# A hybrid decoder block: TensorE takes its instructions in the written order, and four places are rearranged for it

## The chip, the core and the metric

One core of a Trainium2 chip runs the whole block as one program. The metric is the device time of an execution in microseconds (us), lower is better. The kernel before was run three times. One more execution was profiled; its trace gives every instruction of every engine. The engines are TensorE (PE, matrix products), VectorE (DVE), ScalarE (ACT), GpSimd (POOL) and SyncE (SP), which here only issues DMAs.

## The reference

512 tokens of width 2048 get 16 meta tokens ahead of them (528 in all). The block is:

```python
u = rmsnorm(h, norm_g)
q, k, v, g_att, z_ssm, xbc, dt, m_att, m_ssm = split(u @ w_in)
oa = rmsnorm(diff_attention(q, k, v, lam), subln_g) * silu(g_att)   # 8 heads, two softmax maps, a = p0 - lam * p1
y_att = oa @ w_br_attn
xs, bm, cm = split(silu(causal_conv4(xbc) + conv_b))
ys = ssd_chunked(xs, softplus(dt + dt_bias), -exp(a_log), bm, cm)   # 4 groups of 8 heads, chunks of 128 tokens
yg = rmsnorm_per_group((ys + xs * d_skip) * silu(z_ssm))
y_ssm = yg @ w_br_ssm
merged = sigmoid(m_att) * y_att + sigmoid(m_ssm) * y_ssm
out = rmsnorm((h + merged @ w_out)[16:], final_g)
```

All of it is float32.

## The kernel before, in words

**The dense products.** Every weight matrix is cut into jobs of 256 output columns. `plan` (L60-87) writes their order: keys and values of the first head, two merge gates and `dt`; then per head a `kv` and a `qg` job; gates `ma` 2 and on; the conv inputs `bc` and `xs`; per SSD group two `z` jobs and two to six gates, the last of them `ms` 7; then eight jobs each of `ya` (attention branch), `ys` (SSD branch) and `out`. Each float32 operand is split in a high and a low part (`wh` by ACT at L173, `wl` by DVE at L174, for the weights; `xsplit`, L438 and L439, for the activations), and a product is three matmuls. Most jobs go through `strassen` (L216-322): seven products P1 to P7 of half-sized blocks in place of eight, two units each, 12 matmuls of 256 or 264 columns a unit (L310). The sums of weight blocks are made at L184 and L187 on DVE, and the results are put together by "posts" at L187. Jobs of form F go through `plain` (L324-361, matmuls at L354). The activation operands have names, B11, B12, B21, B22 and the sums T1 to T4, and `TOK` says which product reads which; they lie in slots of two pools (eight slots `x`, six slots `y`). Weights come in by DMA, five buffers deep (`pump`, L157-167).

**What sets the order.** `dense` (L400) takes a job's units: sums two units ahead, splits (`prep`) so that up to three prepared units wait, and then the matmuls (`run_unit`, L384). Behind each unit `run_posts` runs what `later` has put off by so many units, and `run_side` (L197) takes one step of each of up to three side tasks, which are generators; in the heads a new one may start every 3 units, in the SSD stage every 10. A head's side tasks are queued 6 units behind its `qg` job. `before={j: f}` runs f ahead of the sums of unit j.

**Side tasks.** Per head: `qk_parts` (L684-695) makes the split queries and keys `qs`, `ks`, `kl` in four steps; `attn_rows` (L698-772) makes scores for four blocks of 128 rows (matmuls L719 with 128 rows of contraction and L722 with 64, written as all L719 of a step, then all L722), softmax (L726 to L756), transposes (L762, L764), and values (L770, L771); `attn_out` (L774-800) normalizes (`og`, L792) and transposes (L796). Between the conv stage and the first `z` job, after a `flush`, stands the SSD set-up (L897-961): it loads `dt` (L913), transposes it (L922, L924), computes softplus and decays in a chain on DVE and ACT (L925-946), sums them along the chunk by matmul (L948, L949), and transposes the sums (L958). Per SSD group, `ssd_group` (L984-1119) runs four chunks with matmuls from L1026 to L1108 (L1067 the state, L1086 the output, L1095 ACT, L1101 and L1108 the norm) and operations on POOL (L178, L190) between them.

**Between the stages.** The last gate job, `ms` 7, splits the attention operands (`att_quarter`, L1123) ahead of its units 8 to 11. While `ya` runs, `ssm_operands` (L1194) makes the seven operands of `ys` from `yq`; T2 and T3 are subtracted on POOL (`psub`, L181), the others on DVE (`vsub`, L184). During the last `ys` job `out_operand` (L1225) starts the operands of `out` from `mq`. `final` (L1301-1330) takes the squares' sums of the finished rows by matmul (L1307), the norm (L1309 POOL), spreads it (L1313) and scales (L1319 DVE). At the start `token_scale` (L510-547) takes the same steps for the input norm, in two halves; the second half's matmul L527 is written behind the first dense unit.

**Who orders the engines.** The kernel is built with a planner that orders each engine's instructions by its own estimate of their times:

```python
with tile.TileContext(nc, schedule_with_timeline_sim=True) as tc:
    block_kernel(tc, t_in, out)
```

An engine then runs its list in the planner's order, and waits for semaphores where another engine's result is needed. An instruction written later can so stand earlier on its engine.

## Time and profile before

| What | Value |
|---|---|
| three runs | 1816.68, 1818.43, 1822.35 us; median 1818.43 |
| profiled execution | 1816.67 us, of which the span of the trace 1815.0 us |
| mean granted clock of TensorE in the span | 0.973 of full speed |
| instructions | PE 13547, DVE 3004, ACT 1961, POOL 241 |
| busy | PE 1707.7 us, DVE 1565.0, ACT 969.2, POOL 262.1 |
| moved by DMA | 244.10 MB |

The span runs from the first to the last instruction that the trace has; all times in it count from its start. Busy time is the time in which an engine executed something other than waiting, branching or issuing a DMA. PEclk is the clock granted to TensorE as a share of full speed: 1.00 is 2.4 GHz, 0.50 is 1.2 GHz. Stages by time, roughly: start to 140 us, heads 140 to 600, gates and conv 600 to 846, SSD with its `z` jobs and gates 846 to 1350, `ya` 1350 to 1450, `ys` 1450 to 1612, `out` to the end.

### The profile page before, as it was taken

What the parts mean: (1) busy time and instruction counts of PE and PEld (TensorE: products, weight loads), DVE (VectorE), ACT (ScalarE), POOL (GpSimd) and SP (SyncE); (2) the same over time, 40 slices, a digit from 0 to 9 for tenths busy, and PEclk for the clock granted to TensorE, in tenths of its full rate; (3) what the DMA queues carried; (4) which work ended last, traced back from release to release, by engine and by line L of the source; (5) the groups of instructions that cost most, each with busy time, mean ns of one, the idle gap of its engine ahead of it and who ended that gap; (6) DMA issues with size and microseconds to landing.
All of it is one profiled execution on the core that took longest, in us unless ns stands there. A gap on an engine that the chain in (4) does not pass through costs nothing.

```text
span 1815.0 us, 35924 instructions
## 1 busy us (share of the span) xinstructions
PE 1707.7 (94%) x13547; PEld 1639.2 (90%) x13547; DVE 1565.0 (86%) x3004; ACT 969.2 (53%) x1961; POOL 262.1 (14%) x241
## 2 busy tenths in 40 slices
PE   5999999999999799999998999999998999989995
PEld 4999988988989799999997889989998999989995
DVE  6898878887888699999988888988978499999996
ACT  6555545554565355555576665555553254455553
POOL 0000000000000000000013431121302012235443
PEclk9999989998999899999999999999999999999998
DMA  7332212221223134333556555455466545433433
GB/s 298 134 113 82 88 64 88 70 89 65 88 76 106 66 129 129 129 118 129 154 172 177 172 156 171 158 169 167 127 231 228 186 144 171 153 114 106 139 117 105
DMA packets 136765, 244.10 MB, mean 134 GB/s; under 512 B 15088, under 2 KB 78768, under 8 KB 136080
## 3 DMA queue, kind: packets, MB, share of 16 engines
q1 hardware_dynamic: 136592, 241.81, 40.9%
q8 instruction: 107, 1.75, 0.4%
q14 instruction: 66, 0.54, 0.1%
HBM read 207.88 MB, written 33.88 MB: 133 GB/s over the span
## 4 chain that ended last, share of the span: by engine, by line
PE 68%; DVE 18%; DMA 5%; issue 4%; ACT 4%; POOL 1%; SPq 0%; DVEq 0%; ACTq 0%; POOLq 0%
PE d_ps L310 53%; PE d_ps L354 6%; DVE wl L174 5%; DMA w<-in_w_all 2%; DVE w L184 2%; DVE cv L865 2%; DMA mm<-d_acs 2%; PE s_ps L722 1%; ACT wh L173 1%; DVE S L187 1%; PE o_ps L770 1%; ACT mm L1049 1%; DVE u L187 1%; PE s_ps L719 1%; DVE S L184 1%
## 5 line engine op out<-in xcount | busy, mean ns | idle before, releaser
L310 PE MATMUL d_ps<-x,wh 128*128 128x256 f32 (+1 forms) x4160 | 772.2, 286 | 16.2 <-ACT x L438 5.9
L310 PEld LDWEIGHTS d_ps<-x,wh 128*128 128x128 f32 x4160 | 647.9, 191 | 24.7 <-ACT x L438 6.3
L173 ACT ACTIVATE wh<-w 128x512 fp32r<-128x512 f32 x706 | 438.3, 628 | 407.1 <-PE d_ps L310 263.0
L310 PE MATMUL d_ps<-x,wl 128*128 128x256 f32 (+1 forms) x2080 | 593.1, 287 | 11.1 <-DVE wl L174 10.7
L174 DVE TENSOR_TENSOR wl<-w,wh 128x512 fp32r<-128x512 f32 x706 | 506.5, 729 | 109.7 <-ACT wh L173 105.5
L310 PE MATMUL d_ps<-y,wh 128*128 128x256 f32 (+1 forms) x3120 | 585.8, 287 | 8.4 <-ACT wh L173 5.2
L310 PEld LDWEIGHTS d_ps<-y,wh 128*128 128x128 f32 x3120 | 488.3, 191 | 18.9 <-ACT wh L173 8.0
L310 PE MATMUL d_ps<-y,wl 128*128 128x256 f32 (+1 forms) x1560 | 444.4, 287 | 0.6 <-DVE wl L174 0.5
L310 PEld LDWEIGHTS d_ps<-x,wl 128*128 128x128 f32 x2080 | 393.7, 190 | 17.9 <-DVE wl L174 15.0
L310 PEld LDWEIGHTS d_ps<-y,wl 128*128 128x128 f32 x1560 | 296.1, 191 | 3.9 <-DVE wl L174 1.7
L173 ACT ACTIVATE wh<-S 128x512 fp32r<-128x512 f32 x260 | 158.7, 627 | 154.6 <-PE d_ps L310 73.5
L174 DVE TENSOR_TENSOR wl<-S,wh 128x512 fp32r<-128x512 f32 x260 | 182.3, 716 | 23.6 <-ACT wh L173 21.5
L354 PE MATMUL d_ps<-x,wh 128*128 128x256 f32 x704 | 129.3, 284 | 2.1 <-DVE cth L1170 1.1
L354 PEld LDWEIGHTS d_ps<-x,wh 128*128 128x128 f32 x704 | 109.5, 191 | 3.3 <-ACT y L438 1.3
L354 PE MATMUL d_ps<-x,wl 128*128 128x256 f32 x352 | 99.2, 286 | 5.5 <-DVE wl L174 5.4
L184 DVE TENSOR_TENSOR S<-S,w 128x512 f32<-128x512 f32 x130 | 94.6, 766 | 0.0
L184 DVE TENSOR_TENSOR w<-w 128x512 f32<-128x512 f32 x130 | 92.3, 719 | 0.0
L184 DVE TENSOR_TENSOR w<-w,S 128x512 f32<-128x512 f32 x130 | 88.3, 693 | 1.1
L187 DVE TENSOR_TENSOR S<-w 128x512 f32<-128x512 f32 x130 | 86.8, 707 | 2.4 <-DMA w<-in_w_all 2.0
L789 POOL TENSOR_TENSOR ssq<-ssq,mhalf 128x4 f32<-128x4 f32 x8 | 8.1, 1007 | 514.2 <-DVE ssq L788 514.2
L354 PEld LDWEIGHTS d_ps<-x,wl 128*128 128x128 f32 x352 | 66.4, 190 | 6.6 <-DVE wl L174 6.2
L190 POOL TENSOR_TENSOR mq<-mq,cth 128x256 f32<-128x256 f32 x32 | 36.5, 1152 | 194.5 <-DVE mq L187 191.0
(258 smaller groups left out, 1849.2 us busy)
## 6 DMA issues: line engine op xcount, KB each, us to landing
w<-in_w_all SPq DMA_DIRECT2D x291, 512.0 KB, 3.6
mm<-d_acs SPq DMA_DIRECT2D x16, 512.0 KB, 6.5
d_x<-cv SPq DMA_DIRECT2D x24, 264.0 KB, 2.0
q_B<-in_xT SPq DMA_DIRECT2D x8, 528.0 KB, 11.8
d_tha<-gth SPq DMA_DIRECT2D x16, 256.0 KB, 3.1
lx<-d_x SPq DMA_DIRECT2D x16, 256.0 KB, 4.5
d_sz<-gth SPq DMA_DIRECT2D x16, 256.0 KB, 4.3
lz<-d_sz SPq DMA_DIRECT2D x16, 256.0 KB, 3.5
```

Source lines behind the costliest of these rows:

```text
L173: act.activation(h[:, :n], src, AF.Copy)
L174: dve.tensor_tensor(l[:, :n], src, h[:, :n].bitcast(F32), ALU.subtract)
L184: dve.tensor_tensor(dst, a, b, ALU.subtract)
L187: dve.tensor_tensor(dst, a, b, ALU.add)
L190: pool.tensor_tensor(dst, a, b, ALU.mult)
L310: pe.matmul(ps[:, :width], lhsT=a[:, ks], rhs=x[:, kk, lo:lo + width], start=(kk == 0 and i == 0), stop=(kk == kp - 1 and i == 2))
L354: pe.matmul(b[:, :width], lhsT=a[:, cs], rhs=x[:, ki, lo:lo + width], start=(first and k == 0 and i == 0), stop=(last and k == 1 and i == 2))
L719: pe.matmul(ps[:, :b - a], lhsT=qs[:, m, rows], rhs=ks[:, m, a:b], start=True, stop=False)
L722: pe.matmul(ps[:, :b - a], lhsT=qs[ms, m, rows], rhs=kl[ms, a:b], start=False, stop=True)
L770: pe.matmul(o_ps[:, i, :], lhsT=at[:, j, :], rhs=vt[:, j, :], start=(j == 0), stop=False)
L865: dve.scalar_tensor_tensor(v, raw[:, j:j + L], cw[:, ft, j:j + 1], v, ALU.mult, ALU.add)
L1049: act.activation(mm[:, h, :], mm[:, h, :], AF.Relu, scale=-1.0, bias=acs[:, c, g * HPG + h:g * HPG + h + 1])
```

## The change

Every instruction that the kernel writes for TensorE goes through a wrapper, `InOrder`, which adds an edge from the instruction written before it on TensorE. The edge is one of order alone: it has no semaphore and no wait, and binds the planner to keep TensorE's list as written. The other engines stay free. Further:

- `qk_parts` makes `ks` first, then `kl`, and the low parts of `qs` last; `later(after, 4)` queues a head's side tasks two units sooner.
- The last gate job takes its products in the order `ORDER_LAST`, and the input's slots are handed out in the order B11, B21, B22, so that the slots of B11 and B21 are free sooner for the attention operands.
- In a `z` job the buffer of the tanh is taken with the tanh (`squash`), and for the first tile's second half both come two units later.
- `ssm_operands` makes T2 and T3 on DVE, and B21 and B22 only in `ys` job 0 (`ssm_late`, ahead of its units 1 to 4). `out_operand` makes T2 and T3 on DVE, all low parts on DVE, and swaps the pools of B21 and T3.

```diff
--- before.py
+++ after.py
@@ -49,6 +49,8 @@
 
 ORDER_FIRST = ("P1", "P2")
 ORDER_REST = ("P6", "P7", "P4", "P3", "P5")
+
+ORDER_LAST = ("P1", "P2", "P6", "P7", "P4", "P3", "P5")
@@ -113,10 +115,29 @@
     return np.ascontiguousarray(np.concatenate(out, axis=0))
 
 
+class InOrder:
+
+
+    def __init__(self, tc, engine):
+        self.tc, self.engine, self.last = tc, engine, None
+
+    def __getattr__(self, name):
+        op = getattr(self.engine, name)
+
+        def issue(*args, **kw):
+            r = op(*args, **kw)
+            if self.last is not None:
+                self.tc.add_manual_dep(r.ins, self.last, mybir.DependencyInfo(
+                    mybir.DependencyClass.NoSync, mybir.DependencyReason.DATA), reason="in order")
+            self.last = r.ins.name
+            return r
+        return issue
+
+
 @with_exitstack
 def block_kernel(ctx, tc, t_in, out):
     nc = tc.nc
-    act, dve, pool, pe, sp = nc.scalar, nc.vector, nc.gpsimd, nc.tensor, nc.sync
+    act, dve, pool, pe, sp = (nc.scalar, nc.vector, nc.gpsimd, InOrder(tc, nc.tensor), nc.sync)
     wd = t_in["w_all"]
     jobs = plan()
 
@@ -213,7 +234,7 @@
 
     parity = [0]
 
-    def strassen(ji, width, lo, dst, fin, end=None, first=None):
+    def strassen(ji, width, lo, dst, fin, end=None, first=None, order=ORDER):
 
 
 
@@ -316,7 +337,7 @@
             src = ahead if part is ORDER_FIRST else block
             return (lambda: sums(p, u)), (lambda: prep(p, u, src)), (lambda hl: mm(p, u, *hl))
 
-        for part in (ORDER,) if first is None else (ORDER_FIRST, ORDER_REST):
+        for part in (order,) if first is None else (ORDER_FIRST, ORDER_REST):
             for p in part:
                 for u in range(nu):
                     yield unit(p, u, part)
@@ -386,7 +407,7 @@
         mm(hl)
         run_posts()
         if after is not None:
-            later(after, 6)
+            later(after, 4)
         if beside:
             for _ in range(pace["steps"]):
                 run_side()
@@ -454,7 +475,7 @@
     xw = [xslot(xb, "x", (1, D))[:, 0].bitcast(F32) for _ in range(2)]
     xw += [xslot(xt, "y", (1, D))[:, 0].bitcast(F32) for _ in range(2)]
     rb = xslot(xt, "y", (2, HL)).bitcast(F32)
-    for v in ("B11", "B22", "B21"):
+    for v in ("B11", "B21", "B22"):
         xv[v] = tuple(xslot(xb, "x", (8, HL)) for _ in range(2))
     xv["B12"] = tuple(xslot(xt, "y", (8, HL)) for _ in range(2))
     mw = wp.tile([P, 1024], F32, tag="S", bufs=1, name="S")
@@ -564,7 +585,7 @@
         return [(t[:, 8 * n:8 * n + 8], 0, 8), (t[:, M + 256 * n:M + 256 * (n + 1)], 8, HL)]
 
 
-    def gate_job(name, idx, spill):
+    def gate_job(name, idx, spill, order=ORDER):
         th = {}
 
         def dst(f, n):
@@ -579,7 +600,7 @@
                 if n == 1:
                     sp.dma_start(spill[2 * idx + f], th[f])
             later(squash, 1)
-        return strassen(job_at[name, idx], 256, 8, dst, fin)
+        return strassen(job_at[name, idx], 256, 8, dst, fin, order=order)
 
 
     def plain_gate(idx):
@@ -681,18 +702,18 @@
 
         lo_, hi_ = slice(0, 64), slice(64, 128)
         scale = -0.125 * 2.0 ** (hd + 1)
+        act.activation(ks[lo_, 0], kT[lo_], AF.Copy)
+        act.activation(ks[hi_, 1], kT[hi_], AF.Copy)
         act.activation(qs[lo_, 0], qT[lo_], AF.Copy, scale=scale)
         act.activation(qs[hi_, 1], qT[hi_], AF.Copy, scale=scale)
-        yield
-        dve.scalar_tensor_tensor(qs[hi_, 0], qT[lo_], scale, qs[lo_, 0].bitcast(F32), ALU.mult, ALU.subtract)
-        dve.scalar_tensor_tensor(qs[lo_, 1], qT[hi_], scale, qs[hi_, 1].bitcast(F32), ALU.mult, ALU.subtract)
-        act.activation(ks[lo_, 0], kT[lo_], AF.Copy)
-        act.activation(ks[hi_, 1], kT[hi_], AF.Copy)
         yield
         dve.tensor_tensor(kl[lo_], kT[lo_], ks[lo_, 0].bitcast(F32), ALU.subtract)
         dve.tensor_tensor(kl[hi_], kT[hi_], ks[hi_, 1].bitcast(F32), ALU.subtract)
         act.activation(ks[hi_, 0], kT[lo_], AF.Copy)
         act.activation(ks[lo_, 1], kT[hi_], AF.Copy)
+        yield
+        dve.scalar_tensor_tensor(qs[hi_, 0], qT[lo_], scale, qs[lo_, 0].bitcast(F32), ALU.mult, ALU.subtract)
+        dve.scalar_tensor_tensor(qs[lo_, 1], qT[hi_], scale, qs[hi_, 1].bitcast(F32), ALU.mult, ALU.subtract)
         yield
 
     def attn_rows(hd, i, qs, ks, kl, vt, hs):
@@ -971,14 +992,16 @@
             return sz[f][:, 256 * n:256 * (n + 1)]
 
         def fin(f, n, d):
-            t = sb.tile([P, 256], F32, tag="zt", bufs=1, name="zt")
-
-            def gated():
+            def squash():
+                t = sb.tile([P, 256], F32, tag="zt", bufs=1, name="zt")
+                act.activation(t, d, AF.Tanh, scale=0.5)
+                later(lambda: gated(t))
+
+            def gated(t):
                 dve.scalar_tensor_tensor(d, t, 1.0, d, ALU.add, ALU.mult)
                 if n == 1:
                     sp.dma_start(d_sz[2 * idx + f], sz[f])
-            act.activation(t, d, AF.Tanh, scale=0.5)
-            later(gated)
+            later(squash, 2 if (f, n) == (0, 1) else 0)
         return strassen(job_at["z", idx], 256, 8, dst, fin)
 
     def ssd_group(g):
@@ -1146,7 +1169,7 @@
         oq[v] = yst.tile([P, 4, 256], F32, name=f"oq{v}")
         sp.dma_start(oq[v], d_oa[kh, t])
     name, i = rest[-1]
-    dense(gate_job(name, i, d_ths), before={8 + j: (lambda v=v: att_quarter(v))
+    dense(gate_job(name, i, d_ths, ORDER_LAST), before={8 + j: (lambda v=v: att_quarter(v))
                                             for j, v in enumerate(("B11", "B12", "B21", "B22"))})
     flush()
     xv.update(xatt)
@@ -1202,15 +1225,23 @@
                 yield
         y11, y12, y22, y21 = qs
         for v, d, (p, m) in (("B11", y11, (None, None)), ("T1", y11, (y12, y11)), ("T2", y11, (y22, y11)),
-                             ("T3", y12, (y22, y12)), ("T4", y11, (y21, y11)), ("B21", y21, (None, None)),
-                             ("B22", y22, (None, None))):
+                             ("T3", y12, (y22, y12)), ("T4", y11, (y21, y11))):
             if v not in xy:
                 xy[v] = tuple(xslot(xb, "x", (8, 256)) for _ in range(2))
             for o in parts:
                 if p is not None:
-                    (psub if v in ("T3", "T2") else vsub)(d[:, o], p[:, o], m[:, o])
+                    vsub(d[:, o], p[:, o], m[:, o])
                 xsplit(xy[v], d[:, o], o)
                 yield
+        yq.update(B21=y21, B22=y22)
+
+    def ssm_late(v, o):
+
+        if v not in xv or xv[v] is not xy.get(v):
+            xv[v] = xy[v] = tuple(xslot(xb, "x", (8, 256)) for _ in range(2))
+        xsplit(xy[v], yq[v][:, o], o)
+
+    yq = {}
     prep_ys = ssm_operands()
     tasks.append(prep_ys)
     for i in range(8):
@@ -1225,20 +1256,22 @@
     def out_operand(v, *parts):
 
         if v not in xo:
-            xo[v] = tuple(xslot(yp, "y", (8, 256)) if v in ("B11", "B12", "B21", "T4") else xslot(xb, "x", (8, 256))
+            xo[v] = tuple(xslot(yp, "y", (8, 256)) if v in ("B11", "B12", "T3", "T4") else xslot(xb, "x", (8, 256))
                           for _ in range(2))
         d, p, m = {"B11": (m11, None, None), "B12": (m12, None, None), "B21": (m21, None, None),
                    "B22": (m22, None, None), "T1": (m11, m12, m11), "T2": (m11, m22, m11),
                    "T3": (m12, m22, m12), "T4": (m11, m21, m11)}[v]
         for o in parts:
             if p is not None:
-                (psub if v in ("T2", "T3") else vsub)(d[:, o], p[:, o], m[:, o])
-            xsplit(xo[v], d[:, o], o, pool if v == "B22" and o.start == 0 and p is None else dve)
+                vsub(d[:, o], p[:, o], m[:, o])
+            xsplit(xo[v], d[:, o], o)
 
     QV = ("B11", "B12", "B21", "B22")
     early = {7 + 2 * j: (lambda v=v: out_operand(v, slice(0, 3), slice(3, 6))) for j, v in enumerate(QV)}
+    soon = {1 + 2 * j + k: (lambda v=v, k=k: ssm_late(v, slice(4 * k, 4 * k + 4)))
+            for j, v in enumerate(("B21", "B22")) for k in range(2)}
     for i in range(8):
-        dense(ys_job(i, mq), before=early if i == 7 else None)
+        dense(ys_job(i, mq), before=soon if i == 0 else early if i == 7 else None)
     flush()
     for v in QV:
         out_operand(v, slice(6, 8))
```

## Rows read from the trace of the kernel before

**Rows 1.** The page, part 1: busy us, share of the span, instructions.

```profile
PE 1707.7 (94%) x13547; PEld 1639.2 (90%) x13547; DVE 1565.0 (86%) x3004; ACT 969.2 (53%) x1961; POOL 262.1 (14%) x241
```

**Rows 2.** The table by stage: start:end and length, busy us of each engine (instructions), PEclk, DMA.

```profile
140.00:585.00 445.00, 430.43 (x3164) 397.46 (x3164) 358.40 (x882) 236.01 (x532) 7.05 (x7) 0.96 0.24 81
585.00:640.00 55.00, 43.20 (x312) 41.16 (x311) 37.76 (x88) 21.90 (x45) 1.40 (x7) 0.84 0.24 83
640.00:845.00 205.00, 199.11 (x1627) 197.01 (x1626) 205.00 (x397) 107.96 (x181) 1.81 (x18) 1.00 0.37 125
880.00:1340.00 460.00, 442.51 (x3614) 419.52 (x3613) 412.62 (x760) 283.58 (x647) 110.22 (x92) 0.99 0.55 166
1340.00:1400.00 60.00, 52.44 (x414) 51.38 (x414) 46.58 (x58) 27.04 (x43) 10.91 (x4) 0.94 0.65 229
...
1480.00:1600.00 120.00, 120.00 (x1003) 120.00 (x1002) 114.88 (x198) 55.30 (x91) 28.31 (x24) 1.00 0.47 157
...
1600.00:1660.00 60.00, 49.72 (x379) 48.43 (x378) 59.40 (x71) 31.70 (x52) 25.82 (x14) 0.91 0.32 107
```

**Rows 3.** The same table, of two stretches at the lower clock.

```profile
251.20:261.40 10.20, 8.53 (x29) 6.64 (x30) 4.37 (x17) 2.04 (x7) 0.53 (x1) 0.50 0.08 26
596.00:613.10 17.10, 9.05 (x37) 8.16 (x38) 4.52 (x14) 2.00 (x10) 1.20 (x5) 0.50 0.06 19
```

**Rows 4.** The waits of PE: what waited for what, us in total, times, longest.

```profile
PE s_ps L796 <- DVE og L792: 15.9, 6, 4.2
...
PE s_ps L1307 <- DVE sqa L187: 6.8, 1, 6.8
```

**Rows 5.** Timeline of PE in a head: start us, us from start to last end, instruction.

```profile
325.14 0.53 PE L719 MATMUL s_ps<-ks,qs 128*128 128x400 f32 x2
325.60 0.45 PE L722 MATMUL s_ps<-kl,qs 64*128 64x400 f32 x2
...
335.95 0.48 PE L719 MATMUL s_ps<-ks,qs 128*128 128x512 f32 x1
336.36 0.49 PE L722 MATMUL s_ps<-kl,qs 64*128 64x512 f32 x1
```

**Rows 6.** Timeline of PE where the conv stage ends.

```profile
845.71 0.40 PE L310 MATMUL d_ps<-x,wh 128*128 128x256 f32 x2
```

**Rows 7.** Instructions of lines 922 and 948: ns min/median/max, first and last start.

```profile
L922 PE MATMUL s_ps<-ident,mm x1: 193/193/193, 866.6 to 866.6; 32*16 32x32 f32 x1
...
L948 PE MATMUL s_ps<-dec,tri x2: 298/298/299, 914.3 to 914.4; 128*128 128x160 f32 x2
```

**Rows 8.** Groups by form, 840 to 920: names, shapes, count, busy us, mean ns, idle before.

```profile
L865 DVE SCALAR_TENSOR_TENSOR cv<-raw,c_conv_w,cv 128x528 f32<-128x528 f32 x6 | 4.4, 772 | 0.0
...
L937 DVE SCALAR_TENSOR_TENSOR acs<-acs,dec 128x160 f32<-128x160 f32 x7 | 2.2, 320 | 0.0
```

**Rows 9.** DMA issues, 840 to 920: count, KB each, us to landing.

```profile
d_x<-cv SPq DMA_DIRECT2D x2, 264.0 KB, 2.3
...
mm<-d_dt SPq DMA_DIRECT2D x1, 66.0 KB, 2.0
```

**Rows 10.** Timeline of DVE at the start of ya.

```profile
1366.40 1.22 DVE L184 TENSOR_TENSOR yq<-yq 128x1024 f32<-128x1024 f32 x1
...
1368.47 3.43 DVE L184 TENSOR_TENSOR yq<-yq 128x1024 f32<-128x1024 f32 x1
```

**Rows 11.** Groups by form on POOL in the SSD stage.

```profile
L178 POOL TENSOR_TENSOR y<-y,lx 128x512 f32<-128x512 f32 x16 | 25.8, 1612 | 84.4 <-issue 31.0 <-DVE y L1089 29.9 <-DMA ea<-d_acs 8.8
L190 POOL TENSOR_TENSOR lz<-y,lz 128x512 f32<-128x512 f32 x16 | 25.2, 1575 | 17.1 <-DMA lz<-d_sz 16.1
L178 POOL TENSOR_TENSOR y<-y 128x256 f32<-128x256 f32 x16 | 21.3, 1330 | 48.7 <-ACT y L1095 48.7
```

**Rows 12.** Timeline of PE at the program's start.

```profile
31.61 0.61 PE L527 MATMUL s_ps<-ident,r 128*128 128x128 f32 x4
```

## The prediction, made before the changed kernel was run

> **What bounds the kernel now.** I read the busy times first. TensorE (PE) is busy 1707.7 of 1815.0 us and VectorE (DVE) 86% [rows 1]: TensorE is the bound, and what can be won is its 107 us of idle time, the time at the lower clock, and matmuls that are slow because of their neighbours. The table by stage shows where these lie [rows 2]: span less PE busy is idle time, and one less PEclk, times the span, is what the clock cost. Heads (140 to 585): 14.6 us idle, about 17 of clock. Their end (585 to 640): 11.8 and 8.8. SSD (880 to 1340): 17.5 and 5 to 7. Start of `ya` (1340 to 1400): 7.6 and 3.6. Start of `out` (1600 to 1660): 10.3 and 5.4. The conv stage is different: DVE is busy 205.0 of 205.0, so no order of TensorE's matters there. The third view is two stretches in which the granted clock was 0.50, the 1.2 GHz level [rows 3]; they follow idle time on TensorE, so every stall costs about as much again. The fourth, the waits, says what the stalls are: the largest is L796 waiting for `og` of DVE, 15.9 us in 6, up to 4.2 [rows 4]. L796 belongs to a side task, and every dense matmul behind it on TensorE waits too, though nothing of its own is late.
>
> Durations are of the profiled execution: span 1815.0, 1816.67 with what lies around it, 1.76 below the median of 1818.43. Under 0.3%, 5.5 us, a change can't be told from none.
>
> **The change, part by part.** The edges make TensorE follow the order in which the kernel's loops write. The planner now departs from that: it lets prepared dense units pass side matmuls.
>
> *Heads.* Side matmuls now run late and in lumps; the written order spreads them, a step behind each unit. I take the 14.6 us idle and 17 of clock as gained: **+32**. What is late next is DVE: 358.4 us of work in 445 [rows 2]; with 32 us and the score order's 12 gone, in about 401, or 89%. A step with 12 to 15 us of DVE work behind 9 to 12 us of matmuls (my count of five to seven units) now stalls TensorE where before it let other units pass. Bounds: nothing, if the three units prepared ahead (12 matmuls each, 120 us / 1003 = 0.12 us a matmul [rows 2], so 4.3 us) always cover it, and 4.2 us a head, the largest such wait in the rows [rows 4]. I take 2 a head, the middle, as the burst is about 3 us too long in some places and covered in others: **-16** (0 to -34).
>
> *Reordered* `qk_parts`. The same instructions, so it costs nothing; it brings the `ks` and `kl` that the first score needs ahead of the `qs` lows. Its cover is the dense unit between two steps; without it, one subtraction a head, about the 0.77 us of L865, as wide [rows 8].
>
> *Score order.* Written are two L719 (128 rows), then two L722 (64 rows). The trace has mostly L719, L722, L719, L722. Where two L719 stand together, 400 columns each, they take 325.60 - 325.14 = 0.46 us, 0.23 each; an L719 of 512 columns ahead of an L722 takes 336.36 - 335.95 = 0.41 [rows 5], where 512 columns by the first rate would take about 0.29. So each switch between the shapes shows 0.12 to 0.2 us. Per group of four, two switches go; 40 groups (80 L719 in all), about 0.3 each: **+12** (5 to 16).
> Here a rule speaks against: the Trainium skill, "TensorE: Matmul & The Clock Gate", Part 3, The mechanism, says that a weight load overlaps running matmuls only where their row groups differ. By that, two L719 in a row would expose their loads, and this term would be about zero or negative, the sum 12 us worse. The 0.23 us for 400 columns [rows 5] does not agree.
>
> *End of the heads.* 11.8 idle and 8.8 clock [rows 2, 3]; the last head's side steps have little dense work behind them and start two units earlier (`later(after, 4)`). Some L796 wait stays: I leave 4.6 of the 20.6: **+16** (8 to 20).
>
> *SSD set-up.* The costliest loss. Written, L922/L924, L948/L949 and L958 all stand ahead of the first `z` job. In the trace the first `z` matmul, 256 columns, runs at 845.71 [rows 6], right behind the conv's last one, while L922 runs at 866.6 and L948 at 914.3 [rows 7]. With the order held, `z` waits for: the conv's last posts and gating, three taps of 0.77 for each of two tiles [rows 8], 4.6, and about 3 for the posts, activations and gating around them; a landing of `d_x` that frees the conv's buffers, 2.3, and then, four constants later on the same queue (about 2), one of `mm<-d_dt`, 2.0 [rows 9]; a chain of some 23 small operations on ScalarE and DVE at the 0.32 of L937 [rows 8], 7.4; and two trips over TensorE, about 2. Together 23 us idle, and about 3 for the clock as the work starts again (an estimate; the 10.2 us at half clock of [rows 3] cost 5): **-26**. Bounds: 9, if the load comes earlier and only the 7.4 and the trips count, and 30. I take the sum, as the loads' queue (SP) is kept in order too and nothing in the change touches this part.
>
> *SSD chunks.* Idle 17.5 and clock about 7 [rows 2]; 21 of it gained. But a chunk's chain L1086, L1089, then on GpSimd (POOL) 1.61 and 1.58, L1095, 1.33 and a last short one, L1101 [rows 11], takes about 7 us, and the written order lets five units (5 x 12 x 0.12 = 7.2 us) pass between. DVE's queue decides: 0 to 1.8 us a chunk, 16 chunks. I take 0.8: **+21 - 13** (0 to -29). The `z` squash two units later is a ScalarE instruction out of the way of `wh` and costs nothing, since `wh` is three units ahead; without that cover it is one narrow activation a job, under the 0.77 of L865 at half its width.
>
> *Start of `ya`.* DVE's subtraction of 1024 columns takes 1.22 us alone (1366.40) and 3.43 (1368.47) beside one of GpSimd's [rows 10]. The change takes T2 and T3 off GpSimd, so four stretched DVE operations lose 2.2 us each and four of 1.22 are added, takes B21 and B22 out to `ys` job 0, and frees the slots of B11 and B21 by `ORDER_LAST` and the slot order, so that the attention operands are split earlier. The 11.2 us there are mostly gained: **+9** (5 to 11).
>
> *`ys` and `out`.* Job 0 of `ys` gets four late splits on a DVE that is busy 114.88 of 120 [rows 2]: **-3** (0 to -5). The `out` operands go through the same exchange, and DVE gets two subtractions in parts (4 x 1.22) and the B22 split (0.9 by its 768 columns), while B21 no longer waits for T1's slot until `ys` is over. Of 15.7 us [rows 2] I take 11 gained, and 6 lost to DVE: **+5** (-3 to 12).
>
> *Program start.* The second token scaling's L527 runs at 31.61, behind four units [rows 12]; written, it stands behind one, and its input comes from GpSimd not long before 31.6. Units 1 to 3, 4.3 us at full clock and more at the half clock of the start, wait: **-4.5** (-2 to -6). *End.* The first L1307 stands between two units and waits 1.5 us more; the 6.8 us wait [rows 4] behind DVE's scaling may shrink by as much: **-1.5** (-4 to +2).
>
> **The sum.** Gains 32 + 12 + 16 + 21 + 9 + 5 = 95. Losses 16 + 26 + 13 + 3 + 4.5 + 1.5 = 64. Net -31: 1816.67 becomes 1785.7; with 1.76 to the median, **1787 us**.
>
> **Rivals.**
> *Slower: DVE's lumps in the heads.* The written order puts a head's scores, softmax and transposes at fixed places; if DVE reaches `og` 4.1 us late in every head, TensorE stops at L796 each time and drops to half clock for 10.2 us as it did from 251.2 [rows 3], 4.2 + 5.1 = 9.3 a head, 74 in eight. That is 58 more than my 16: 1845. It decides from 31 + 16 = 47 us, or 6 a head. For it: DVE at 89%. Against: the six such waits of now come to 2.65 on the mean [rows 4], in spite of late side work.
> *Cancels.* The losses come at the upper end of two of the three unknown chains (SSD chunks -29, heads -30): 1787 + 30 = 1817, no change.
> *Larger gain.* DVE keeps ahead in heads and chunks, so that the 16 and the 13 go: 1758. For it: the units prepared ahead. Against: DVE at 89%.
> *The edges do next to nothing*, because the planner's order is nearly the written one; only `ya`, `ys` and `out` act: 1818.4 - 9 - 5 + 3 = 1807. Against it: L948 at 914.2 instead of ahead of 845.71 [rows 6].
>
> **How the numbers follow.** Forecast 0.50, larger gain 0.15, edges do nothing 0.07: faster 0.72. Cancels: same 0.11. Slower 0.17. The range reaches from the larger gain, 1758, to a little beyond "cancels", 1822; outside lie the lump case and sums of good ends.
>
> **What would show it.** Right: idle time on TensorE of about 20 us between the conv's last matmul and the first `z`; L719 twice in a row; no half clock after 613; a `ya` start without 3.4 us subtractions; waits at L796 of 1 to 3 us a head. Wrong: idle time in the heads above 6 us each, with the clock at 0.50 in them; a first `z` at once behind the conv (a gain of 26 more); PE waiting for `wl` all through `ys`.

## The result and the profile after

The changed kernel takes 1892.33 us (median of 4 runs, 1891.09 to 1895.22) against 1818.55 us: ratio 1.0405, 95% interval 1.0385 to 1.0426. It is **74 us slower**, where 1787 us were forecast, and lies outside the range.

In the profile after, every TensorE instruction has line L128, as the wrapper issues it; it is told by its tiles (`s_ps<-ks` is L719 of before, `s_ps<-kl` L722, `n_ps<-ones` L1101, `s_ps<-ident,og` L796). Other lines have moved on: `wl` L174 to L195, the eight Relu activations that stand ahead of a chunk's exponential L1049 to L1072 (the exponential itself is L1074), the square L1095 to L1118, POOL's addition and product L178 and L190 to L199 and L211.

Busy times on the page of the profile after, then its table by stage, with the columns of [rows 2]:

```profile
PE 1702.0 (90%) x13547; PEld 1647.6 (87%) x13547; DVE 1578.6 (84%) x3013; ACT 972.1 (51%) x1961; POOL 229.3 (12%) x232
```

```profile
140.00:580.00 440.00, 412.24 (x3170) 386.65 (x3169) 366.14 (x906) 236.09 (x543) 10.34 (x8) 0.99 0.25 82
580.00:640.00 60.00, 59.37 (x482) 59.16 (x482) 55.39 (x107) 29.53 (x50) 0.60 (x8) 0.98 0.37 119
833.00:866.00 33.00, 9.15 (x59) 8.45 (x59) 18.56 (x45) 8.36 (x17) 0.50 (x2) 0.64 0.24 64
866.00:1420.00 554.00, 480.25 (x3790) 460.96 (x3789) 442.86 (x777) 298.24 (x661) 95.90 (x92) 0.93 0.47 144
```

TensorE's work is the same, 13547 instructions, and its busy time is 5.7 us less than in [rows 1]. The span is 75.0 us longer (1890.0 against 1815.0), all of it idle time. The heads and their end have improved: the clock is 0.99 and 0.98 where [rows 2] has 0.96 and 0.84. The SSD stage is where it went wrong: 74 us idle and a clock of 0.93, against 17.5 and 0.99. (The two windows differ in length; over the same dense matmuls, 5400 to 8600 of the table below, it is 73.8 us idle against 18.3, and 482.7 us busy against 467.6.)

To put a number on each stage, the start of the same dense matmul, counted from the program's start, is compared in the two traces:

| Up to | before, us | after, us | behind by | this stage |
|---|---|---|---|---|
| first head (dense matmul 800) | 141.4 | 151.1 | 9.8 | +9.8 |
| behind the heads (3600) | 627.8 | 614.2 | -13.6 | -23.4 |
| conv, last job (5200) | 829.0 | 816.9 | -12.1 | +1.5 |
| first `z` job (5400) | 853.9 | 869.3 | 15.4 | +27.5 |
| last gate job (8600) | 1339.8 | 1425.7 | 85.9 | +70.5 |
| `ya` (9200) | 1422.4 | 1504.6 | 82.2 | -3.7 |
| `ys` (10600) | 1590.4 | 1672.6 | 82.2 | 0.0 |
| `out` (11200) | 1677.2 | 1752.9 | 75.7 | -6.5 |
| end of the span | 1815.0 | 1890.0 | 75.0 | -0.7 |

The waits of PE in the profile after (us in total, times, longest) name what stands behind the two large terms:

```profile
PE n_ps L128 <- POOL y L199: 70.1, 15, 7.1
PE s_ps L128 <- POOL r L544: 16.5, 2, 13.2
PE s_ps L128 <- DMA lx<-d_x: 15.5, 1, 15.5
PE s_ps L128 <- DVE og L813: 13.1, 8, 3.4
PE s_ps L128 <- DVE sc L777: 12.2, 8, 1.5
...
PE s_ps L128 <- DVE dec L967: 7.9, 1, 7.9
```

The first line is new: a chunk's norm matmul waits for POOL's reduction, in 15 of 16 chunks. In before the same wait came to 4.6 us. The third and the sixth are the SSD set-up, 23.4 us together. (For the third the trace names the `lx` load; the matmul reads the `dt` load, issued next to it.) The set-up is seen best in PE's timeline where the conv stage ends, to be held against [rows 6, 7]:

```profile
832.75 0.28 PE L128 MATMUL d_ps<-x,wl 128*128 128x264 f32 x1
848.53 0.63 PE L128 MATMUL s_ps<-ident,mm 32*16 32x32 f32 x5 [15.50 <-DMA lx<-d_x]
857.10 0.87 PE L128 MATMUL s_ps<-dec,tri 128*128 128x160 f32 x2 [7.93 <-DVE dec L967]
857.77 0.74 PE L128 MATMUL s_ps<-dec,ones 128*128 128x160 f32 x2
858.92 1.03 PE L128 MATMUL s_ps<-ident,acs 128*32 128x128 f32 x4 [0.42 <-DVE acs L971]
859.61 0.78 PE L128 MATMUL d_ps<-x,wh 128*128 128x256 f32 x2
```

The first `z` matmul stands last, 26.9 us behind the conv's last one, with 23.9 idle.

**A chunk's wait, followed back.** ACT in the profile after, around the first long wait of the SSD stage:

```profile
941.59 0.62 ACT L194 ACTIVATE wh<-S 128x512 fp32r<-128x512 f32 x1
946.04 0.40 ACT L1072 ACTIVATE mm<-mm,acs 128x128 f32<-128x128 f32 x1 [3.83 <-DMA mm<-d_acs]
946.35 0.61 ACT L194 ACTIVATE wh<-S 128x512 fp32r<-128x512 f32 x1
946.87 2.14 ACT L1072 ACTIVATE mm<-mm,acs 128x128 f32<-128x128 f32 x7
948.91 0.40 ACT L598 ACTIVATE gth<-gth 128x256 f32<-128x256 f32 x1
949.22 0.61 ACT L194 ACTIVATE wh<-w 128x512 fp32r<-128x512 f32 x1
949.74 0.40 ACT L598 ACTIVATE gth<-gth 128x256 f32<-128x256 f32 x1
950.04 0.61 ACT L194 ACTIVATE wh<-w 128x512 fp32r<-128x512 f32 x1
950.57 0.61 ACT L1118 ACTIVATE y<-lz 128x512 f32<-128x512 f32 x1
```

POOL, and then PE, over the same stretch:

```profile
944.56 1.62 POOL L211 TENSOR_TENSOR lz<-y,lz 128x512 f32<-128x512 f32 x1
951.26 1.35 POOL L199 TENSOR_TENSOR y<-y 128x256 f32<-128x256 f32 x2 [5.08 <-ACT y L1118]
```

```profile
952.66 0.59 PE L128 MATMUL n_ps<-ones,y 128*128 128x1 f32 x2 [5.64 <-POOL y L199]
```

DVE, with the first operation of the chain, L1112, behind the last of the dense units' operations that ran ahead of it:

```profile
941.78 0.68 DVE L205 TENSOR_TENSOR w<-w 128x512 f32<-128x512 f32 x1
942.38 0.68 DVE L1112 TENSOR_TENSOR y<-s_ps,y 128x512 f32<-128x512 f32 x1
```

And SP's, with the load that ACT waits for:

```profile
939.75 0.38 SPq L1028 DMA_DIRECT2D mm<-d_acs  x1
```

This chunk's last output matmul ends at 939.72, and DVE takes its sum, L1112, at 942.38, behind operations of the dense units. POOL's product is there at 946.18. The square that reads it runs on ACT at 950.57, as ACT's list has the eight activations L1072 ahead of it, and three splits and two squashes of dense units: by their starts each of the two takes about half of the 4.4 us. The L1072 belong to the chunk two later: its `mm` shares a buffer with this chunk's, the load was issued at 939.75, as this chunk's last output matmul freed it, and landed 6.3 us later. ACT stood still for 3.83 us of that. TensorE had no other work to do by then: between the chunk's last output matmul and its norm matmul the kernel writes 60 dense matmuls (five units of 12; one starts before the output matmul has ended), 7.1 us.

Measured so for all 16 chunks, from the end of a chunk's last output matmul to the start of its norm matmul:

| Kernel | least, us | median, us | most, us | dense matmuls between | square behind POOL's product, median us | the same, sum of 16 | DVE's L1112 behind the last output matmul, sum of 16 |
|---|---|---|---|---|---|---|---|
| before | 9.9 | 18.2 | 54.5 | 60 to 418 | 2.6 | 37.5 | 102.6 |
| after | 7.1 | 11.8 | 14.4 | 60 | 4.0 | 51.9 | 34.8 |
| x11, below | 7.6 | 9.5 | 11.4 | 60 | 1.4 | 22.9 | 23.9 |

So a chunk of after waits for a turn twice, 3.2 us on ACT and 2.2 on DVE on the mean; the operations themselves and the steps from one to the next take the remaining 6.3. In 13 of the 14 chunks that have a chunk two later, the eight L1072 run ahead of the square; the one in which they don't is the one chunk that does not wait, at 7.1 us, and DVE was only 0.2 us late there. In before they ran ahead of the square in all 14 too, and it cost little there (4.6 us of waits), as TensorE had other dense work to run.

### The profile page after: what moved, and what is told of

It reads as the page before. It is cut to its first block, busy times and chain, and to the rows that moved or that the text cites. A ratio compares the mean times of both kernels' runs of the same rounds, so it can differ in the third digit from the quotient of the medians.

```text
span 1890.0 us, 35855 instructions
## 1 busy us (share of the span) xinstructions
PE 1702.0 (90%) x13547; PEld 1647.6 (87%) x13547; DVE 1578.6 (84%) x3013; ACT 972.1 (51%) x1961; POOL 229.3 (12%) x232
## 4 chain that ended last, share of the span: by engine, by line
PE 68%; DVE 16%; DMA 5%; ACT 5%; issue 4%; POOL 1%; SPq 0%; DVEq 0%; ACTq 0%; POOLq 0%
PE d_ps L128 60%; PE s_ps L128 6%; DVE wl L195 4%; DMA mm<-d_acs 3%; ACT mm L1072 2%; DVE w L205 2%; DVE S L208 2%; DVE cv L886 1%; PE o_ps L128 1%; POOL y L199 1%; ACT wh L194 1%; DVE cv L889 1%; DVE u L208 1%; DVE q_B L562 1%; PE n_ps L128 1%
## 5 line engine op out<-in xcount | busy, mean ns | idle before, releaser
L128 PE MATMUL d_ps<-x,wh 128*128 128x256 f32 (+1 forms) x4896 | 927.0, 290 | 17.1 <-DVE x L460 4.3
L128 PEld LDWEIGHTS d_ps<-x,wh 128*128 128x128 f32 x4896 | 776.7, 194 | 32.6 <-issue 8.3
L128 PE MATMUL d_ps<-x,wl 128*128 128x256 f32 (+1 forms) x2448 | 702.7, 287 | 11.6 <-DVE wl L195 11.3
L195 DVE TENSOR_TENSOR wl<-w,wh 128x512 fp32r<-128x512 f32 x706 | 502.9, 721 | 124.6 <-ACT wh L194 122.4
L128 PE MATMUL d_ps<-y,wh 128*128 128x256 f32 (+1 forms) x3216 | 600.4, 287 | 2.6 <-DVE y L460 2.3
L128 PEld LDWEIGHTS d_ps<-y,wh 128*128 128x128 f32 x3216 | 499.9, 190 | 10.5 <-issue 4.8
L128 PEld LDWEIGHTS d_ps<-x,wl 128*128 128x128 f32 x2448 | 473.7, 194 | 14.6 <-DVE wl L195 14.5
L128 PE MATMUL d_ps<-y,wl 128*128 128x256 f32 (+1 forms) x1608 | 456.2, 284 | 0.3 <-DVE wl L195 0.2
L128 PEld LDWEIGHTS d_ps<-y,wl 128*128 128x128 f32 x1608 | 306.2, 190 | 0.9 <-DVE wl L195 0.9
L195 DVE TENSOR_TENSOR wl<-S,wh 128x512 fp32r<-128x512 f32 x260 | 180.9, 712 | 32.0 <-ACT wh L194 29.8
L211 POOL TENSOR_TENSOR mq<-mq,cth 128x256 f32<-128x256 f32 x32 | 44.3, 1396 | 267.6 <-DMA w<-in_w_all 150.7
L128 PE MATMUL n_ps<-ones,y 128*128 128x1 f32 x32 | 8.4, 330 | 70.1 <-POOL y L199 70.1
L128 PEld LDWEIGHTS n_ps<-ones,y 128*128 128x128 f32 x32 | 7.0, 273 | 73.2 <-POOL y L199 73.2
L208 DVE TENSOR_TENSOR u<-d_ps,u 128x256 f32<-128x256 f32 (+1 forms) x130 | 54.5, 419 | 9.2 <-PE d_ps L128 8.8
L1072 ACT ACTIVATE mm<-mm,acs 128x128 f32<-128x128 f32 x128 | 39.8, 389 | 37.4 <-DMA mm<-d_acs 37.4
## 6 DMA issues: line engine op xcount, KB each, us to landing
q_B<-in_xT SPq DMA_DIRECT2D x8, 528.0 KB, 11.8
```

The source lines that it names most:

```text
L128: r = op(*args, **kw)
L195: dve.tensor_tensor(l[:, :n], src, h[:, :n].bitcast(F32), ALU.subtract)
L208: dve.tensor_tensor(dst, a, b, ALU.add)
L211: pool.tensor_tensor(dst, a, b, ALU.mult)
L1072: act.activation(mm[:, h, :], mm[:, h, :], AF.Relu, scale=-1.0, bias=acs[:, c, g * HPG + h:g * HPG + h + 1])
```

## The experiments

The theory from this reading: the rearrangements gain a little, the written order gains in the heads, and loses 27.5 us in the set-up and 70 in the chunks. Rivals: the rearrangements themselves cost; the engines beside TensorE limit the SSD stage in any order; POOL is the chain; or only the written places of the chain's operations are wrong.

**x1_edges_off.** The rearrangements alone:

```diff
-(nc.scalar, nc.vector, nc.gpsimd, InOrder(tc, nc.tensor), nc.sync)
+(nc.scalar, nc.vector, nc.gpsimd, nc.tensor, nc.sync)
```

> The changed kernel without the edges: the planner orders TensorE again, and the rearrangements of operands, slots, the z squash and the scores' operands stay. Theory (the loss of 74 us is that of the written order in the SSD stage; the rearrangements gain a little at the starts of ya and out): 1808 us, 1800 to 1815. Rival A (the rearrangements themselves cost, above all the z squash and the subtractions on DVE): 1840 us or more.

Measured: 1802.81 us, ratio 0.9922 (0.9907 to 0.9936). Rival A falls: the rearrangements gain 0.8%, and all of the loss, and more, comes with the edges.

**x2_ssd_free.** The wrapper gets a switch, off from the set-up to the end of the SSD stage:

```diff
+            if not self.on:
+                return r
...
+    pe.on = False
     ps = side_ps()
...
     sctx.close()
+    pe.on = True
```

> The edges are left out from the first matmul of the SSD set-up to the end of the SSD stage, and stay everywhere else. Theory: the idle 23 us of the set-up and the waits of the chunks' norm matmuls for POOL go; by the stage times of the two traces 27.5 + 71 us come back: 1794 us, 1788 to 1802, below the kernel before. Rival A (z squash two units later costs in this stage): 1830 us or more.

Measured: 1788.26 us, ratio 0.9844 (0.9829 to 0.9859). The table by stage of this run, over its SSD stage:

```profile
837.00:1330.00 493.00, 477.86 (x3937) 454.70 (x3936) 454.04 (x837) 306.21 (x695) 113.69 (x94) 0.99 0.56 170
```

15 us idle and a clock of 0.99. So the edges cost 104 us from the set-up to the end of this stage (1892.33 - 1788.26) and gain 14.5 elsewhere (1802.81 - 1788.26).

**x3_norm_later.** Four more steps ahead of the norm matmul:

```diff
             padd(y[:, :P], y[:, :P], y[:, P:256])
             yield
+            yield
+            yield
+            yield
+            yield
```

> All edges stay; each SSD chunk gets four more units between its reductions on POOL and its norm matmul. Theory (the matmul stops TensorE because 59 dense matmuls, 7.1 us, are written between the chunk's last output matmul and it, while its input takes 11 to 13 us; at nine units, 12.9 us, it is there): 70 us of idle time go and most of the 39 us that the lower clock costs there: 1797 us, 1790 to 1815. Rival B (the engines beside TensorE are the limit of the stage, so the stall moves to the next wait, as the next chunk's output matmul): 1850 us or more, with waits of the same sum at another line.

Measured: 1831.02 us, ratio 1.0076 (1.0061 to 1.0091): 61 us of the 74, between the two expectations. Waits of PE:

```profile
PE n_ps L128 <- POOL sq L1132: 8.1, 4, 2.5
```

The wait for POOL's reduction is gone from the list, and no other has its size, so rival B falls as the main cause. The stage now takes 5.6 us more than before (dense matmuls 5400 to 8600), against 70.5. The expected gain was too large for two reasons. Over those matmuls the idle time fell from 73.8 to 25.9 us, 48 and not 70, as smaller waits took part of its place (the line shown, and those for `wh`, 11.2 us in the whole run against 3.4): so much of rival B is true. And the clock was priced at 39 us from PEclk over the whole stage, where the busy time fell by 17 us only, 482.7 to 465.6. Of the 70.5 us that the changed kernel lost in the stage, 55.5 are idle time (73.8 less 18.3) and the other 15 are longer busy time, at a lower clock.

**x4_square_dve.** The square goes to DVE:

```diff
-            act.activation(y, gz.rearrange("p f t -> p (f t)"), AF.Square)
+            dve.tensor_tensor(y.rearrange("p (f t) -> p f t", f=4), gz, gz, ALU.mult)
```

> All edges stay; the square of a chunk's gated output is taken by DVE, not by ACT. Theory (of the chain's 11 to 13 us some 4 are the square's wait on ACT behind the next chunk's exponentials, which wait for their own load): the chain falls to about 9 us, the stall from 5 to 2 us a chunk in 12 of 16 chunks: 36 us of idle time and about 20 of clock: 1836 us, 1820 to 1852. Rival C (POOL's two passes and two reductions are the chain, and the square would only wait elsewhere): 1885 to 1895 us.

Measured: 1878.55 us, ratio 1.0350 (1.0330 to 1.0371). A miss for both, nearer to rival C:

```profile
PE n_ps L128 <- POOL y L199: 52.7, 16, 5.7
```

On DVE the square waits too: it starts 2.0 to 3.7 us behind POOL's product in every chunk, 42.1 us in all against 51.9 on ACT.

**x5_setup_free.** The switch off for the matmuls of the set-up alone.

```diff
+    pe.on = False
     ps = side_ps()
     pe.transpose(ps[:M, 0:32], dtx[:, :M], ident[:32, :32])
...
     sp.dma_start(d_acs, acT)
+    pe.on = True
```

> The changed kernel with the matmuls and transposes of the SSD set-up alone (transposes of dt, sums along the chunk, transposes of the sums) outside the edges. Theory (with the order held, TensorE stands still through the chain of posts, DMAs and small operations): the 27.5 us that the two traces differ by at that place come back: 1865 us, 1858 to 1872, and the first z matmul follows the conv's last one at once. Rival D (the chunks then start sooner against the same engines and their stalls grow by what was won): 1885 us or more.

Measured: 1869.98 us, ratio 1.0286 (1.0263 to 1.0309), 22 us below the changed kernel. PE's timeline at the conv's end:

```profile
834.57 0.28 PE L128 MATMUL d_ps<-x,wl 128*128 128x264 f32 x1
834.69 0.40 PE L128 MATMUL d_ps<-x,wh 128*128 128x256 f32 x2
```

`z` follows the conv at once, as in [rows 6]. The theory of the set-up holds. From the conv's last job to the first `z` job it takes 24.5 us, where before took 24.9 and the changed kernel 52.4. That 22 and not 27.5 us come back in all is in part one wait, in the SSD stage, that the planner's place for the set-up's sums brings:

```profile
PE s_ps L128 <- DVE dec L970: 6.5, 1, 6.5
```

**x6_before_edges.** The kernel before with the wrapper and nothing else:

```diff
-    act, dve, pool, pe, sp = nc.scalar, nc.vector, nc.gpsimd, nc.tensor, nc.sync
+    act, dve, pool, pe, sp = (nc.scalar, nc.vector, nc.gpsimd, InOrder(tc, nc.tensor), nc.sync)
```

> The kernel before with the edges alone, none of the rearrangements. Theory (the edges cost where side work is late, and the rearranged operands of ya and out and the scores' operands are such places, so without them their stalls come on top): 1920 to 1950 us. Rival E (the rearrangements are worth the same with edges as without, 13 to 16 us): 1905 to 1910. If it is below 1892, the rearrangements harm under the edges.

Measured: 1933.93 us, ratio 1.0636 (1.0615 to 1.0657). The rearrangements are worth 42 us under the edges (1933.93 - 1892.33) and 13 to 16 without. Waits of PE:

```profile
PE n_ps L126 <- POOL y L197: 60.5, 11, 8.8
PE s_ps L126 <- DVE sc L775: 28.5, 8, 3.6
...
PE n_ps L126 <- ACT wh L192: 16.2, 4, 4.2
```

The wait at `sc`, 3.6 us a head, falls to 1.5 in the changed kernel. The rearrangements do make room for the written order, most of it in the heads; the chunks' waits are there with them and without, 76.7 us in their two lines here, 70.1 in the changed kernel. By the start of the same dense matmuls:

| Stage, us | before | edges alone (x6) | rearrangements alone (x1) | both (after) |
|---|---|---|---|---|
| heads (800 to 3600) | 486.4 | 481.1 | 478.8 | 463.0 |
| SSD stage (5400 to 8600) | 485.9 | 566.3 | 482.1 | 556.4 |
| `ya` (8600 to 9200) | 82.6 | 87.2 | 81.1 | 78.9 |
| `out` (10600 to 11200) | 86.8 | 87.2 | 82.1 | 80.3 |

The edges pay in the heads, together with the rearrangements. At `ya` and `out` most of the gain is the rearrangements' own.

**x7_three_mends.** x3 and x5 together, and the switch off for the second token scaling.

```diff
     def second():
+        pe.on = False
         token_scale(1)
+        pe.on = True
```

> The changed kernel with three mends of the written order: the norm matmul of a chunk four units later, the set-up's matmuls outside the edges, and the second token scaling's matmul outside the edges too. Theory (these three places are the whole loss, each for itself): 1831 as measured with the later norm, less 27.5 for the set-up, less about 6 of the 9 us lost before the first head: 1797 us, 1788 to 1806. Rival D (they depend on each other, the time moves to the next wait): 1815 or more.

Measured: 1808.31 us, ratio 0.9944 (0.9923 to 0.9964). The time lies between the two expectations. Three places mended turn 4.1% slower into 0.6% faster. The start gave only about 2 of the 6 us: at dense matmul 400 the run is 7.5 us behind before, x3 9.3.

**x8_ssd_start_free.** x2 with the same switch at the start.

> No edges from the SSD set-up to the end of the SSD stage, nor on the second token scaling's matmul; edges elsewhere. Theory (the order as written is good in the heads, at ya and at out, and bad in the SSD stage and at the start): 1788 as measured without edges in the SSD stage, less about 6: 1782 us, 1776 to 1787.

Measured: 1786.54 us, ratio 0.9825 (0.9804 to 0.9847), the same as x2. The second L527 is therefore only a small part of the loss at the start: at dense matmul 400 the run is still 8.1 us behind before. Up to 105 us its PE waits 14.7 us for the split activations `x` and `y`; in before, and in x10 below without edges there, such waits come to 7.5 and 7.6.

**x9_chain_early.** TensorE's order stays; the chain's later operations are written earlier:

```diff
             pmul(gz, y.rearrange("p (f t) -> p f t", f=4), gz)
-            yield
-            yield
-
             act.activation(y, gz.rearrange("p f t -> p (f t)"), AF.Square)
-            yield
             padd(y[:, :256], y[:, :256], y[:, 256:])
             padd(y[:, :P], y[:, :P], y[:, P:256])
+            yield
+            yield
+            yield
             yield
```

> All edges stay and TensorE's order is that of the changed kernel; a chunk's square on ACT and its two reductions on POOL are written two and three units earlier, right behind the product on POOL, with the same number of steps up to the norm matmul. Theory F (a chunk's operations wait in the queues of ACT and POOL behind the splits of units that are written ahead of them, so their place in the written order is what makes the chain 11 to 13 us): the square follows the product within a microsecond, the chain falls to about 9 us, the stall from 5 to 2 us a chunk, some 60 us with the clock: 1830 us, 1815 to 1850. Rival C (the chain's own operations and DVE's queue ahead of its first one are the length): 1880 to 1892.

Measured: 1894.35 us, ratio 1.0432 (1.0403 to 1.0460). Waits of PE:

```profile
PE n_ps L128 <- POOL y L199: 70.0, 15, 7.0
```

Nothing moved, the square follows the product by 3.9 us in the median as by 4.0, so theory F falls: written two and three units earlier, the operations kept the places that the planner gives them.

**x10_heads_start.** x2, the switch off for the whole start too, and a step more at the two places in the heads where TensorE waits:

```diff
         dve.scalar_tensor_tensor(a[:, :n], pr[1][:, :n], cc, a[:, :n], ALU.mult, ALU.add)
         yield
+        if i == 2:
+            yield
...
         dve.tensor_tensor(og, o_ps, r0.unsqueeze(2).to_broadcast([P, NT, P]), ALU.mult)
         yield
+        yield
```

> No edges ahead of the heads and none in the SSD stage; in the heads, with edges, one more unit ahead of the transposes of the third block of rows and one ahead of those of the normalized output, the two places where TensorE waits 1.5 and 1.4 us in each head. Theory (each wait there is short of its input by less than a unit, 1.4 us, so one unit removes it): 1786.5 as measured, less 8 at the start and 16 to 20 of the 25 us in the heads: 1760 us, 1753 to 1770. Rival G (DVE is the limit in the heads, the waits move to the next scores or to wl): 1775 to 1782.

Measured: **1768.56 us, ratio 0.9741 (0.9720 to 0.9762)**, the fastest of all. At dense matmul 400 it is 1.2 us ahead of before, so the start's loss is the edges' as a whole. Waits of PE:

```profile
PE s_ps L128 <- DVE mn L751: 16.7, 8, 2.2
...
PE s_ps L128 <- DVE og L819: 3.4, 1, 3.4
```

The step at `og` does what it should, 13.1 to 3.4 us. The one at `sc` moves the wait to `mn`, 2.1 us a head: half of rival G. So the heads give 8.8 us on x8 (463.0 to 454.2 between dense matmuls 800 and 3600), not 16 to 20. The start gives 9.3, and the two are the 18 us between the runs. The written order, kept where it pays and left where it doesn't, so gains 47.6 us on the kernel before, together with the rearrangements, which gain 13 to 16 of it by themselves.

**x11_square_first.** All edges, and one kind more, on ACT: the square of a chunk ahead of the eight activations of the chunk two later. The expectation calls them exponentials; they are the Relus ahead of the exponential.

```diff
+    sqd = []
...
+                    if len(sqd) > 1:
+                        tc.add_manual_dep(r.ins, sqd[-2], mybir.DependencyInfo(
+                            mybir.DependencyClass.NoSync, mybir.DependencyReason.DATA), reason="square first")
...
-            act.activation(y, gz.rearrange("p f t -> p (f t)"), AF.Square)
+            sqd.append(act.activation(y, gz.rearrange("p f t -> p (f t)"), AF.Square).ins.name)
```

> The changed kernel with one more edge of order, on ACT: a chunk's square stands ahead of the eight exponentials of the chunk two later, which share its operand's buffer and are not needed for 20 us. Theory H (those exponentials, and the wait for their load ahead of them, are what holds the square for about 4 us in 12 of the 16 chunks): the square starts within about 1 us of POOL's product, the chain falls to about 9 us, the stall from 5 to 2: 1840 us, 1825 to 1860. Rival P (ACT's list has other work of the dense units ahead of the square too, the squashes and splits that become ready only as TensorE gets there, so the square's place is late with or without the exponentials): the square still starts about 10 us after the chunk's last output matmul, 1875 to 1892.

Measured: 1849.54 us, ratio 1.0171 (1.0154 to 1.0188). ACT's timeline (the square is L1123 here, the Relus L1074), then PE's wait:

```profile
952.18 0.40 ACT L599 ACTIVATE gth<-gth 128x256 f32<-128x256 f32 x1
952.49 0.61 ACT L1123 ACTIVATE y<-lz 128x512 f32<-128x512 f32 x1
953.01 2.43 ACT L1074 ACTIVATE mm<-mm,acs 128x128 f32<-128x128 f32 x8
```

```profile
PE n_ps L128 <- POOL y L199: 30.4, 16, 3.6
```

One kind of edge between ACT operations wins 43 us, without touching TensorE's order or the work. Theory H holds: those activations and the load ahead of them were more than half of the chunks' loss (70.1 us of waits fall to 30.4). By the table of the chunks, ACT's queue gave back 29.0 us and DVE's 10.9, which was not aimed at. What is left is of two parts of one size: the square still waits 22.9 us on ACT, which is rival P (in the chunk shown, a squash L599 of a dense unit stands ahead of it), and L1112 23.9 us on DVE, which neither theory named.

**x13_chain_dve.** The four POOL operations of the chain go to DVE:

```diff
-            padd(y, y, xT.rearrange("p f t -> p (f t)"))
-            pmul(gz, y.rearrange("p (f t) -> p f t", f=4), gz)
+            vadd(y, y, xT.rearrange("p f t -> p (f t)"))
+            dve.tensor_tensor(gz, y.rearrange("p (f t) -> p f t", f=4), gz, ALU.mult)
...
-            padd(y[:, :256], y[:, :256], y[:, 256:])
-            padd(y[:, :P], y[:, :P], y[:, P:256])
+            vadd(y[:, :256], y[:, :256], y[:, 256:])
+            vadd(y[:, :P], y[:, :P], y[:, P:256])
```

> All edges stay; the four operations of a chunk's chain on POOL (the addition, the product, the two reductions) go to DVE, where 512 columns take 0.68 us and not 1.3 to 1.6; the square stays on ACT. Theory R (POOL's 5 us are the part of the chain that exceeds the 7.1 us of dense matmuls): the chain falls to 7 us or less, the stalls go: 1805 us, 1795 to 1820. Rival P (the queues in front of each operation are the length: each new operation on DVE waits behind the splits of the dense units as the square did when DVE took it): stalls of 3 us or more remain, 1860 or more.

Measured: 1902.40 us, ratio 1.0464 (1.0443 to 1.0485), 10 us slower still. Waits of PE:

```profile
PE n_ps L128 <- DVE y L208: 39.2, 7, 7.2
PE n_ps L128 <- ACT gth L599: 24.5, 4, 6.3
...
PE n_ps L128 <- ACT zt L997: 11.0, 3, 6.1
```

Operations of half the length, and no less waiting, 74.7 us in the three lines: theory R falls. The addition and the product, 0.68 us each, start 4 us apart in the first chunk (947.10 and 951.13), as DVE's list has a weight split between them that waits 2.42 us for ACT, and one more operation. What the chain takes beyond its operations is the queues in front of them.

## Why the prediction was wrong

The sum was -31 and the span gave +75.0, 106 us apart. By its own steps:

- **The step that failed: "SSD chunks", +21 - 13.** It added up a chunk's chain from the durations of its operations [rows 11], "about 7 us", held that against five units of 7.2 us, and let only DVE's queue decide, 0 to 1.8 us a chunk. The durations were right (6.3 us with the steps between them). The waits for a turn were not: the square's on ACT was left out and measured 51.9 us in the 16 chunks, 3.2 each; DVE's was under-sized and measured 34.8, 2.2 each and up to 4.8. So the chain takes 7.1 to 14.4 us, 11.8 in the middle, and the stage lost 70.5 us where 8 were to be gained: 79 of the 106. The step asked which operations there are, not when they ran. Its own rows had a warning: POOL idle for 48.7 us ahead of its reductions, until ACT's square [rows 11]. In the profile after (POOL, groups by form, 866 to 1420) it is 63.0:

```profile
L199 POOL TENSOR_TENSOR y<-y 128x256 f32<-128x256 f32 x16 | 13.0, 811 | 63.0 <-ACT y L1118 63.0
```

  And none of before's norm matmuls ran less than 9.9 us behind the last output matmul, or had its input less than 8.7 us behind it, while 60 to 418 dense matmuls filled that time. x11 and x3 show the cause, the one by shortening the chain, the other by giving it time.
- **The start**, 4.5 forecast, 9.8 measured. The step priced L527 alone; x8 against x10 (8.1 us behind before at dense matmul 400, and 1.2 ahead) shows that the order of the other matmuls there costs the most of it.
- **The heads and their end**, 32 + 16 + 12 - 16 = 44 gained by forecast, 23.4 measured. The idle time there went from 26.4 us to 27.8, and the busy time from 460.0 to 435.3. The score order was right. PE's timeline shows two matmuls of one shape in a row; the two of 512 and 16 columns take 0.44 us together, where [rows 5] has 0.41 for the one of 512 alone:

```profile
217.45 0.51 PE L128 MATMUL s_ps<-ks,qs 128*128 128x512 f32 x2
217.89 0.51 PE L128 MATMUL s_ps<-kl,qs 64*128 64x512 f32 x2
```

  From one matmul's start to the next, idle time left out, the scores of all heads take 33.9 us and took 49.6: 16 gained, 12 forecast. Two terms are mis-sized. DVE's lumps: 2 us a head forecast, 13.1 + 12.2 + 2.5 = 27.8 us in eight heads, 3.5 a head, measured, all of the idle time and most of it at the same two places in every head. And the clock: it came back nearly whole (0.99 and 0.98), but with the scores taken out the busy time fell by 9 us, where 17 + 8.8 were counted, as PEclk had been priced over idle time too.
- **The set-up**, 26 forecast, 27.5 measured: right, by the sum as it was worked out (23.9 idle; the rest is the clock and the set-up's own 13 matmuls, which now run there), and x5 shows it as a term by itself.
- **`ya`, `ys`, `out`**: +9, -3 and +5 forecast; 3.7, 0 and 6.5 gained. The start of `ya` has no stretched subtraction left (DVE, groups by form, 1400 to 1500):

```profile
L205 DVE TENSOR_TENSOR yq<-yq 128x1024 f32<-128x1024 f32 x8 | 9.6, 1215 | 0.0
```

  The end: -1.5 forecast, 0.7 gained.

The rival "DVE's lumps in the heads" had the mechanism right, a side matmul held in front of ready dense work, but the wrong stage, and DVE is less than half of the queues that count there: the heads' own waits stayed far under its 6 us a head. "The edges do next to nothing" is refuted by x1. Of the signs named for being right, four came true: 23.9 us between the conv and `z`, two L719 in a row, no stretched subtraction at `ya`, 1.6 us a head at L796. The fifth, no half clock after 613, did not: the granted clock was 0.50 in 13 stretches of the SSD stage. No sign looked at the chunks themselves, so the large term could fail with four of five signs in order.

What stays open: why the planner puts those activations ahead of the square. In x9, with the square written earlier, and in x13, without POOL in the chain, they (in two chunks of x13 six of the eight) stand there still, in 13 and in all of the 14 chunks; the planner's own estimates weren't looked at.

## What to carry to other kernels

Before an engine's order is fixed, measure in the trace how long each held instruction's input really takes from the point that starts it, queues included, and count the work that is written in between: 11.8 us against 7.1 was most of the loss here, and the sum of the durations, 7, did not show it. An order that holds one engine turns every late place on the others into idle time of that engine, so order goes where the measured distance is large enough (here the heads, and there with the rearrangements), and stays free, or gets more distance, where it isn't. If a chain is late because of its turn on a shared engine, an edge on that engine can be worth more than faster operations: 43 us gained by the one, 10 lost by the other, in this kernel.

## What the runs showed that had not been expected

- An engine's list can hold ready work behind a load that nobody needs yet. The waits of ACT over the SSD stage of the changed kernel show 37.4 us for it; the activations that start at 946.04 serve output matmuls that run at 989.3:

```profile
ACT mm L1072 <- DMA mm<-d_acs: 37.4, 15, 5.0
```

- The granted clock's price is smaller than PEclk over a stage says: 0.93 over 554 us would be 39 us, but only 15 of the stage's 70.5 us were longer busy time; the rest was idle time, waiting for other engines. So the prediction's "every stall costs about as much again" did not hold here either: 70.1 us of chunk waits came with 15 us.
